# Selected and local attention: the weights turned by TensorE instead of a second pass of scores

## The chip, the cores and the metric

One core of one Trainium2 chip runs the program once. The metric is the time of one execution on the device in microseconds, shown as the median of several runs. One more execution was taken with the hardware profiler; every row below comes from it.

## The reference, cut to what matters

Two transformer blocks follow one another (1024 tokens, width 1024). The first has three mixers: a linear recurrence over 8 heads, a sparse attention with three branches over 4 heads, and an attention over 256 memory rows. The second has retention, a convolution and 64 experts of which each token takes two. The change lies in the sparse attention. With 16 blocks of 64 keys and a top-k of 16, every block is chosen, so the selected branch is causal attention over all earlier keys; the local branch sees the last 512 keys.

```python
s_s = jnp.einsum('bqhd,bqkd->bhqk', qr, kg) * scale
p_s = masked_softmax(s_s, (kpos <= tq[None, :, None])[:, None])
o_s = jnp.einsum('bhqk,bqkd->bqhd', p_s.astype(vg.dtype), vg)
...
m_w = (diff >= 0) & (diff < WINDOW) & (wpos[None, :] >= 0)
s_w = jnp.einsum('bqhd,bkd->bhqk', qr, kwb) * scale
p_w = masked_softmax(s_w, m_w)
o_w = jnp.einsum('bhqk,bkd->bqhd', p_w.astype(vwb.dtype), vwb)
...
o = g[..., 0:1] * o_c + g[..., 1:2] * o_s + g[..., 2:3] * o_w
```

Here 4 heads share one key and value head of 64, and the softmax takes off the largest score of its row.

## The kernel before, in words

The work is staged by halves of the sequence (H is 0 or 1, 512 tokens each). `weave` (L1595) draws from several generators; each `yield` gives a cost, each stream has a rate, and the stream that is furthest behind goes next. Inside a stage the framework then orders each engine's instructions by when it expects them to be ready. L1631 to L1634 weave the projections of the second half with `recur(0)` and `attend(0)`; L1637 weaves `third_stage(0)` (output projection, normalisation, the second block's mixer) with `recur(1)` and `attend(1)`. After them come the second half's output projection and mixer, the router, and the experts, whose weights stream from memory.

`attend` (L1096) takes 4 query tiles of 128 tokens: `mem_tile`, then `nsa_tile` (L947). Values and keys are kept as a float32r high part and a rest: 64 + 64 partitions of `ksT` and `kwT`, 64 + 64 columns of `vsw`; the queries are split into `qh` and `ql` of full value. In `nsa_tile`, per branch (`br`, 0 selected, 1 local) over the key blocks of 128 up to the diagonal (query tile i has i + 1 selected and at most 5 local ones):

- **First pass**, per head and per piece of up to four blocks (`cut`; 5 to 8 blocks make two pieces): scores `pmx` of 128 queries by up to 512 keys (L1012, L1013, masks L1015, L1017), the row's maximum (L1019, DVE), an exponential written back into the same PSUM bank of which only the row sum is kept (L1020, ACT). 96 tiles.
- **Turning the maxima**: 8 maxima per query go through a transpose (`pmr`, L1038) into `nms` and, per branch, into `nmb` (L1044).
- **Second pass**, per key block, all four heads at once: scores `pS` again, now 128 keys by 512 (head, query) (L1057, L1058), less the maximum by a product of `ones` and `nmb` (L1059), a mask on diagonal and edge blocks (L1061). ACT takes the exponential twice, as float32r `ph` (L1064) and as float32 `pf` (L1066); DVE takes `pl` = `pf` - `ph` (L1067); TensorE sums both with the values into `poT` (L1050). 66 blocks.
- **Tail** per branch: the two halves of `poT` are added (L1077, L1078), turned back (`pob`, L1082), weighted and added to `o` (L1085, L1086).

All short-lived score tiles (`pmx`, `pmr`, `pS`, `pob`, those of `mem_tile`) come from `S1` (L217), one ring of two PSUM banks; `poT` has one bank (`O1`). `qd`, `pf` and `mem_tile`'s weights share three buffers of tag `acc`.

Of the kernel before, what the change touches and what calls it, by code (L numbers as in the profile page):

```python
# [9 lines left out]
F32 = mybir.dt.float32  # L10
# [33 lines left out]
def _constants():  # L44

    c = {}
# [19 lines left out]
    r = np.arange(16)[:, None]  # L66
    bh = np.arange(8)[None, :]
    c["nsel"] = np.zeros((P, 8))
    c["nsel"][:16] = 1.0 * (r % 8 == bh)
# [3 lines left out]
    c["causalT"], c["edgeT"] = c["causal"].T, c["edge"].T  # L73
# [18 lines left out]
_GROUPS = (("causal", "edge", "causalT", "edgeT", "before", "ones"), ("ncos", "nsin", "tcos", "tsin", "tcaus", "gam"),  # L92
# [13 lines left out]
def body(tc, a, out, stop=None, dbg=None):  # L106
# [47 lines left out]
    def K(name):  # L154
        o, n = _COFF[name]
        return cst[:, o:o + n]
# [8 lines left out]
    causb, edgeb, causTb, edgeTb, beforeb, onesb = [maskb[:, x * P:(x + 1) * P] for x in range(6)]  # L165
# [184 lines left out]
    def put():  # L350
        return tmp1("put", bufs=3)
# [210 lines left out]
    def att_proj(H):  # L562
        ts, cs = slice(TH * H, TH * H + TH), slice(H2 * H, H2 * H + H2)
        if H == 0:
            for x in range(0, 6, 3):
                masks = put()[:, 0:3 * P]
                nc.sync.dma_start(masks, a["cst"][:, _GOFF[0] + x * P:_GOFF[0] + (x + 3) * P])
                nc.vector.tensor_copy(maskb[:, x * P:(x + 3) * P], masks)
# [311 lines left out]
    nsel = K("nsel")[0:16].rearrange("p (b h) -> p b h", b=2)  # L880

    ones = const.tile([P, P], F32R, name="ones")
    nc.vector.tensor_scalar(ones, ident, 0.0, 1.0, op0=OP.mult, op1=OP.add)
    nmb = at.tile([P, 4, P], F32R, tag="nmb", name="nmb")
    nc.vector.tensor_scalar(nmb, ident[:, None, :].to_broadcast([P, 4, P]), 0.0, None, op0=OP.mult)

# [20 lines left out]
    def mem_tile(i):  # L907
# [5 lines left out]
        for e in range(2):  # L913
            ps = S1("pM")
            for c in range(2):
                nc.tensor.matmul(ps[:, c * 256:(c + 1) * 256], mq[lohi[e], c], memk[lohi[e], c], start=True, stop=True)
            nc.vector.tensor_reduce(nm[:, 2 * e:2 * e + 2], ps.rearrange("p (c k) -> p c k", c=2), axis=AX.X, op=OP.max,
                                    negate=True)
            pr = at.tile([P, 2, 256], F32, tag="acc", name="prm", bufs=3)
# [27 lines left out]
    def nsa_tile(i):  # L947
        H = i // TH
        qd = at.tile([P, 4 * P], F32, tag="acc", name="qd", bufs=3)
# [49 lines left out]
        mx = at.tile([P, 2, 4, 2], F32, tag="mx", name="mx")  # L999
        sm = at.tile([P, 2, 4, 2], F32, tag="sm", name="sm")  # L1000
        for br, kT in enumerate((ksT, kwT)):
# [3 lines left out]
            for h in range(4):  # L1005
                q = slice(h * P, (h + 1) * P)
                for n, (u, v) in enumerate(zip(cut, cut[1:])):
                    ps = S1("pmx")
                    w = (v - u) * P
                    ends, starts = v == nb, br == 1 and i >= 4 and u == 0  # L1010
                    rhs = kT[:, (s0 + u) * P:(s0 + v) * P]
                    nc.tensor.matmul(ps[:, 0:w], qh[:, q], rhs, start=True, stop=False)  # L1012
                    nc.tensor.matmul(ps[:, 0:w], ql[:, q], rhs, start=False, stop=not (ends or starts))  # L1013
                    if starts:
                        nc.tensor.matmul(ps[:, 0:P], identb, edgeb, start=False, stop=not ends)  # L1015
                    if ends:
                        nc.tensor.matmul(ps[:, w - P:w], identb, causb, start=False, stop=True)  # L1017
                    m = mx[:, br, h, n:n + 1]
                    nc.vector.tensor_reduce(m, ps[:, 0:w], axis=AX.X, op=OP.max, negate=True)  # L1019
                    nc.scalar.activation(ps[:, 0:w], ps[:, 0:w], AF.Exp, bias=m, accum_out=sm[:, br, h, n:n + 1])  # L1020
                yield 0.25 * nb
            if len(cut) > 2:
                m, mb = at.tile([P, 4], F32, tag="mc", name="m"), mx[:, br]
                nc.vector.tensor_tensor(m, mb[:, :, 0], mb[:, :, 1], op=OP.min)
                nc.vector.tensor_tensor(mb, m[:, :, None].to_broadcast([P, 4, 2]), mb, op=OP.subtract)
                nc.scalar.activation(mb, mb, AF.Exp)
                nc.vector.tensor_tensor(sm[:, br], sm[:, br], mb, op=OP.mult)
                nc.vector.tensor_tensor(sm[:, br, :, 0], sm[:, br, :, 0], sm[:, br, :, 1], op=OP.add)
                nc.vector.tensor_copy(mb[:, :, 0], m)

        mm = at.tile([P, 2, 8], F32R, tag="mm", name="mm")
        mv = mx[:, :, :, 0]
        nc.vector.tensor_copy(mm[:, 0].rearrange("p (b h) -> p b h", b=2), mv)
        nc.vector.tensor_sub(mm[:, 1].rearrange("p (b h) -> p b h", b=2), mv,
                             mm[:, 0].bitcast(F32).rearrange("p (b h) -> p b h", b=2))
        yield 0.2
        pt = S1("pmr")
        nc.tensor.transpose(pt[0:16, 0:P], mm.bitcast(F32).rearrange("p x n -> p (x n)"), ident)  # L1038
        nms = at.tile([16, P], F32, tag="qn", name="nms")
        nc.vector.tensor_copy(nms, pt[0:16, 0:P])  # L1040
        yield 0.204
        for br, kT in enumerate((ksT, kwT)):
            s0 = b0 if br else 0
            nc.vector.tensor_tensor(nmb[0:16], nms[:, None, :].to_broadcast([16, 4, P]),  # L1044
                                    nsel[:, br, :, None].to_broadcast([16, 4, P]), op=OP.mult)
            po = O1("poT")

            def with_v(b, ph, pl):
                for p_ in (ph, pl):
                    nc.tensor.matmul(po, vsw[:, b, br], p_, start=(b == s0 and p_ is ph), stop=(b == i and p_ is pl))  # L1050

            ready = None
            for b in range(s0, i + 1):
                ps = S1("pS")
                blk = kT[:, b * P:(b + 1) * P]
                mask = causTb if b == i else edgeTb if br == 1 and b == i - 4 else None
# [3 lines left out]
                if mask is not None:  # L1060
                    nc.tensor.matmul(ps.rearrange("p (h t) -> p h t", h=4), identb,  # L1061
                                     mask[:, None, :].to_broadcast([P, 4, P]), start=False, stop=True)
                ph = at.tile([P, 4 * P], F32R, tag="ph", name="ph", bufs=2)
                nc.scalar.activation(ph, ps, AF.Exp)  # L1064
                pl, pf = at.tile([P, 4 * P], F32R, tag="pl", name="pl", bufs=2), at.tile([P, 4 * P], F32, tag="acc", name="pf", bufs=3)
                nc.scalar.activation(pf, ps, AF.Exp)  # L1066
                nc.vector.tensor_sub(pl, pf, ph.bitcast(F32))  # L1067
                yield 0.8
                if ready:
                    with_v(*ready)  # L1070
                    yield 0.604
                ready = b, ph, pl
            yield 0.73
            with_v(*ready)
            yield 0.336
            oS = at.tile([P, 4 * P], F32R, tag="pl", name="oS", bufs=2).bitcast(F32)
            nc.scalar.activation(oS[64:P], po[64:P], AF.Copy)  # L1077
            nc.vector.tensor_tensor(oS[0:64], po[0:64], oS[64:P], op=OP.add)  # L1078
            yield 0.153
            pt = S1("pob")  # L1080
            for h in range(4):
                nc.tensor.transpose(pt[:, h * 64:h * 64 + 64], oS[0:64, h * P:(h + 1) * P], ident[0:64, 0:64])  # L1082
            v = pt[:, 0:256].rearrange("p (h d) -> p h d", h=4)
            t = at.tile([P, 4, 64], F32, tag="sqh", name="ob")
            nc.vector.tensor_tensor(t, v, weight(br + 1, sm[:, br, :, 0]), op=OP.mult)  # L1085
            nc.vector.tensor_tensor(o, o, t, op=OP.add)  # L1086
# [92 lines left out]
    def close_first(H, wk, wg=None):  # L1179
# [3 lines left out]
        for i, rr in enumerate(rows):  # L1183
            n = TH * H + i
            nc.vector.scalar_tensor_tensor(rr, rr, row_rs(wk, rr), gf, op0=OP.mult, op1=OP.mult)
# [3 lines left out]
            nc.scalar.activation(rr, rr, AF.Copy, scale=row_rs(wk, rr))  # L1189
# [822 lines left out]
```

## Time and profile before

| what | us |
|---|---|
| median of 3 runs (2540.53 to 2549.47) | 2548.81 |
| the profiled execution, its own time | 2546.94 |
| its span, from the first to the last instruction | 2544.8 |
| PE busy | 2423.5 |
| DVE busy | 1550.0 |
| ACT busy | 772.7 |
| POOL busy | 348.5 |

PE is busy for 95% of the span, but a matmul's row lasts until its modelled end, which overlaps the next one's start. What a matmul takes from the engine's time is therefore read from one start to the next in a timeline. From 1560 us on the experts run, with the DMA engines busy most of the time.

### The profile page before, as it was taken

The page shows a single profiled execution, that of the slowest core. Times are in us where ns is not written, and L with a number is a line of the kernel's source. Part 1 is how long each engine was busy: PE and PEld are TensorE (multiplying, and loading weights), DVE is VectorE, ACT ScalarE, POOL GpSimd, SP SyncE. Part 2 cuts the span into 40 slices and gives each one's busy share as a digit, 9 for nine tenths or more (in the row PEclk, how much of TensorE's full clock was granted, in tenths as well). Part 3 has the DMA queues.
Part 4 walks back from the last instruction along what each step waited for, and adds up shares of the span by engine and source line. Part 5 has one row for each costly group of instructions (what it writes and reads, how often), then busy time and mean ns, then how long its engine had stood idle before and what let it go on. Part 6 is the DMA issues. An engine that isn't in the chain of part 4 may idle for free. (4 is left out here: it accounts for less than half of the span.)

```text
span 2544.8 us, 36038 instructions
## 1 busy us (share of the span) xinstructions
PE 2423.5 (95%) x13518; PEld 1545.9 (61%) x13518; DVE 1550.0 (61%) x3104; ACT 772.7 (30%) x1516; POOL 348.5 (14%) x464
## 2 busy tenths in 40 slices
PE   8989999999988999999999969999999999999997
PEld 6766777777756767887878834444444444444443
DVE  5537666665776776676665646555555555555555
ACT  4423544434436543334242321111111111111112
POOL 3000000000001011101120020111111111111112
PEclk9989999999888999999999979999999999999999
DMA  7666544443523222445345668999999999999992
GB/s 166 163 148 192 144 106 123 109 121 94 177 59 117 73 70 71 133 136 170 116 139 196 248 237 358 410 408 412 412 409 412 410 408 412 410 410 408 408 410 84
DMA packets 352078, 603.67 MB, mean 237 GB/s; under 512 B 124408, under 2 KB 298112, under 8 KB 327328
## 3 DMA queue, kind: packets, MB, share of 16 engines
q1 hardware_dynamic: 344496, 592.53, 64.9%
q0 software_dynamic: 5168, 8.69, 1.1%
q8 instruction: 108, 1.77, 0.3%
q14 instruction: 66, 0.54, 0.1%
q10 hardware_dynamic: 2240, 0.14, 0.1%
HBM read 562.54 MB, written 47.25 MB: 240 GB/s over the span
## 5 line engine op out<-in xcount | busy, mean ns | idle before, releaser
L1738 PE MATMUL pgu<-mw,xT 128*64 128x512 f32 x2048 | 460.9, 597 | 2.3 <-DVE up L1743 2.3
L277 PE MATMUL pcm<-hTh,whi 128*128 128x512 f32 (+1 forms) x912 | 370.1, 406 | 0.2 <-DVE hTl L265 0.2
L277 PE MATMUL pcm<-hTh,wlo 128*128 128x512 f32 (+1 forms) x912 | 362.9, 398 | 0.4 <-DVE wlo L238 0.4
L277 PE MATMUL pcm<-hTl,whi 128*128 128x512 f32 (+1 forms) x912 | 360.8, 396 | 0.0
L237 ACT ACTIVATE whi<-wraw 128x512 fp32r<-128x512 f32 (+1 forms) x300 | 187.2, 625 | 458.8 <-PE pcm L277 318.0
L238 DVE TENSOR_TENSOR wlo<-wraw,whi 128x512 fp32r<-128x512 f32 (+1 forms) x300 | 211.4, 708 | 181.0 <-ACT whi L237 159.2
L1738 PEld LDWEIGHTS pgu<-mw,xT 128*64 128x64 f32 x2048 | 142.7, 137 | 265.6 <-issue 254.7
L1796 DVE TENSOR_TENSOR mw<-psp,mw 128x1024 f32<-128x1024 f32 x248 | 292.5, 1220 | 8.8 <-PE psp L1788 5.1
L1788 PE MATMUL psp<-yo,wt 128*128 128x512 f32 x1024 | 274.9, 410 | 4.1 <-DVE mw L1796 3.2
L1788 PEld LDWEIGHTS psp<-yo,wt 128*128 128x128 f32 x1024 | 182.8, 188 | 139.0 <-issue 80.6
L1766 PE MATMUL pyd<-mw,hT 128*64 128x512 f32 x1008 | 229.9, 598 | 2.3 <-DVEq L1929 2.3
L1742 DVE SCALAR_TENSOR_TENSOR mth<-mth,pgu 64x512 f32<-64x512 f32 x64 | 43.4, 679 | 291.6 <-ACT mth L1741 291.6
L277 PEld LDWEIGHTS pcm<-hTh,whi 128*128 128x128 f32 (+1 forms) x912 | 170.6, 187 | 41.4 <-issue 6.2
L277 PEld LDWEIGHTS pcm<-hTl,whi 128*128 128x128 f32 (+1 forms) x912 | 170.8, 187 | 39.3 <-issue 6.2
L277 PEld LDWEIGHTS pcm<-hTh,wlo 128*128 128x128 f32 (+1 forms) x912 | 170.2, 187 | 40.1 <-issue 2.3
L1741 ACT ACTIVATE mth<-pgu,rq 64x512 f32<-64x512 f32 x64 | 43.8, 684 | 491.8 <-PE pgu L1738 491.8
L1773 ACT ACTIVATE yo<-pyd,gt 64x512 fp32r<-64x512 f32 x128 | 87.6, 684 | 305.6 <-PE pyd L1766 304.3
L1775 DVE SCALAR_TENSOR_TENSOR yo<-pyd,gt,yo 64x512 fp32r<-64x512 f32 x128 | 95.9, 749 | 126.5 <-ACT yo L1773 125.4
L1781 POOL TENSOR_SCALAR wt<-rcon,tfs 128x128 fp32r<-128x128 f32 x256 | 150.3, 608 | 149.1 <-PE psp L1788 125.4
L1766 PEld LDWEIGHTS pyd<-mw,hT 128*64 128x64 f32 x1008 | 66.9, 136 | 126.7 <-issue 123.2
L1800 POOL DMA_INDIRECT xg<-d_x,idxt x32 | 34.4, 1074 | 688.6 <-issue 630.4
L1170 PE MATMUL pout<-whi,yh 128*128 128x512 f32 x256 | 107.7, 421 | 3.0 <-DVE rr L1173 3.0
(492 smaller groups left out, 3464.3 us busy)
## 6 DMA issues: line engine op xcount, KB each, us to landing
mw<-in_w_gate_dram SPq DMA_DIRECT2D x64, 2048.0 KB, 13.7
mw<-in_w_up_dram SPq DMA_DIRECT2D x64, 2048.0 KB, 9.6
mw<-in_w_down_dram SPq DMA_DIRECT2D x63, 2048.0 KB, 14.4
wraw<-in_w_in_dram SPq DMA_DIRECT2D x216, 256.0 KB, 3.2
wraw<-in_w_out_dram SPq DMA_DIRECT2D x32, 256.0 KB, 2.8
yr<-d_y SPq DMA_DIRECT2D x32, 256.0 KB, 3.0
d_x<-rr SPq DMA_DIRECT2D x16, 512.0 KB, 2.8
wraw<-in_w_o_dram SPq DMA_DIRECT2D x32, 256.0 KB, 2.9
```

Source lines behind the costliest of these rows:

```text
L237: nc.scalar.activation(hi, raw, AF.Copy)
L238: nc.vector.tensor_sub(lo, raw, hi.bitcast(F32))
L277: nc.tensor.matmul(ps[0:n], w, h[:, k], start=(k == 0 and j == 0), stop=(k == KD - 1 and j == 2))
L1170: nc.tensor.matmul(ps, y[:, t], w, start=(k == 0 and j == 0), stop=(k == 1 and j == 2))
L1738: nc.tensor.matmul(ph_[lohi[s]], xT[:, k], pieces[s][:, k * 512:(k + 1) * 512], start=(k == 0), stop=(k == KD - 1))
L1741: nc.scalar.activation(th, ph_[0:64], AF.Tanh, scale=rq[:, 0, h:h + 1])
L1766: nc.tensor.matmul(py[s][lohi[s]], hT[:, k, lohi[h]], piece[:, k * 1024 + s * 512:k * 1024 + s * 512 + 512], start=(k == 0), stop=(k == 3))
L1773: nc.scalar.activation(y[:, 0, 512 * s:512 * s + 512], py[s][o], AF.Copy, scale=gt[o, h:h + 1])
L1775: nc.vector.scalar_tensor_tensor(y[:, 1, 512 * s:512 * s + 512], py[s][o], gt[o, h:h + 1], y[:, 0, 512 * s:512 * s + 512].bitcast(F32), op ...
L1781: nc.gpsimd.tensor_scalar(w[0:n, i], iota[0:n], sh[0:n, i:i + 1], None, op0=OP.is_equal)
L1788: nc.tensor.matmul(ps[:, cs], w[0:n], yo[0:n, x, cs], start=(start and x == 0), stop=(x == 1))
L1796: nc.vector.tensor_tensor(x2, ps, x2, op=OP.add)
```

## The change

The second pass goes. Per branch, piece of up to four key blocks and pair of heads, the exponential of the first pass is now kept, as `pr` in SBUF; TensorE turns it, 128x128 at a time and up to four (two key blocks by two heads) to a bank (`pTs`); ACT copies the bank as float32r `ph`, DVE takes `pl` = `pTs` - `ph`; and TensorE sums both with the values into `poT`, 256 columns at a time. Each piece has its own sum; a piece's `poT` is copied whole, turned by four 128x128 transposes, and its two halves are added after that. Where a branch has two pieces, they are weighted by their own maxima at the end. `ones`, `nmb`, `nsel`, the turned masks and the transpose of the maxima go. `acc` has four buffers; the squares of `close_first` write to tag `yl`; the masks come in one load instead of two. Rates in `weave` are as they were.

```diff
-            for x in range(0, 6, 3):
-                masks = put()[:, 0:3 * P]
...
+            masks = put()
+            nc.sync.dma_start(masks, a["cst"][:, _GOFF[0]:_GOFF[1]])
+            nc.vector.tensor_copy(maskb, masks)
...
-    ones = const.tile([P, P], F32R, name="ones")
...
-    nmb = at.tile([P, 4, P], F32R, tag="nmb", name="nmb")
...
-                    nc.scalar.activation(ps[:, 0:w], ps[:, 0:w], AF.Exp, bias=m, accum_out=sm[:, br, h, n:n + 1])
-                yield 0.25 * nb
...
-        nc.tensor.transpose(pt[0:16, 0:P], mm.bitcast(F32).rearrange("p x n -> p (x n)"), ident)
...
-            for b in range(s0, i + 1):
-                ps = S1("pS")
...
-                nc.tensor.matmul(ps, blk, qh, start=True, stop=False)
-                nc.tensor.matmul(ps, blk, ql, start=False, stop=False)
-                nc.tensor.matmul(ps, ones, nmb.rearrange("p h t -> p (h t)"), start=False, stop=mask is None)
...
-                nc.scalar.activation(ph, ps, AF.Exp)
...
-                nc.scalar.activation(pf, ps, AF.Exp)
-                nc.vector.tensor_sub(pl, pf, ph.bitcast(F32))
...
-            nc.scalar.activation(oS[64:P], po[64:P], AF.Copy)
-            nc.vector.tensor_tensor(oS[0:64], po[0:64], oS[64:P], op=OP.add)
...
+            for n, (u, v) in enumerate(zip(cut, cut[1:])):
...
+                po = O1("poT")
+                ready = []
+
+                def with_v():
+                    j, bs, parts = ready.pop(0)
+                    for k, b in enumerate(bs):
+                        for p_ in parts:
+                            nc.tensor.matmul(po[:, 256 * j:256 * j + 256], vsw[:, s0 + u + b, br], p_[:, 256 * k:256 * k + 256],
+                                             start=(b == 0 and p_ is parts[0]), stop=(b == v - u - 1 and p_ is parts[1]))
+                    return 0.302 * len(bs)
+
+                for j in range(2):
+                    prs = []
+                    for h in (2 * j, 2 * j + 1):
...
+                        ps = S1("pS")
...
+                        nc.vector.tensor_reduce(m, ps[:, 0:w], axis=AX.X, op=OP.max, negate=True)
+                        pr = at.tile([P, 4 * P], F32, tag="acc", name="pr", bufs=4)
+                        nc.scalar.activation(pr[:, 0:w], ps[:, 0:w], AF.Exp, bias=m, accum_out=sm[:, br, n, h:h + 1])
+                        prs.append(pr)
...
+                    for g in range(0, v - u, 2):
+                        bs = range(g, min(g + 2, v - u))
+                        pt = S1("pTs")
+                        for k, b in enumerate(bs):
+                            for x in range(2):
+                                nc.tensor.transpose(pt[:, (2 * k + x) * P:(2 * k + x + 1) * P], prs[x][:, b * P:(b + 1) * P],
+                                                    ident)
+                        c = 256 * len(bs)
+                        ph, pl = [at.tile([P, 4 * P], F32R, tag=t, name=t, bufs=2) for t in ("ph", "pl")]
+                        nc.scalar.activation(ph[:, 0:c], pt[:, 0:c], AF.Copy)
+                        nc.vector.tensor_sub(pl[:, 0:c], pt[:, 0:c], ph[:, 0:c].bitcast(F32))
...
+                nc.scalar.activation(oS, po, AF.Copy)
...
+                for h in range(4):
+                    nc.tensor.transpose(pt[:, h * P:(h + 1) * P], oS[:, h * P:(h + 1) * P], ident)
...
+                nc.scalar.activation(t, pt[:, :, 0], AF.Copy)
+                nc.vector.tensor_tensor(t, pt[:, :, 1], t, op=OP.add)
...
+            jk = dict(tag="yl", bufs=4)
+            nc.vector.scalar_tensor_tensor(rr, rr, row_rs(wk, rr, **jk), gf, op0=OP.mult, op1=OP.mult)
```

Counted over the program, TensorE loses 198 float32r products of 512 columns (132 scores, 66 with `ones`), 20 masks of 512, 8 transposes `pmr` and 64 small transposes `pob`; 132 products with the values of 512 columns become 264 of 256; 264 transposes `pTs` and 96 `pob` of 128x128 come in. ACT loses 132 exponentials and 16 half copies, and gets 78 copies `ph` (54 of 512 columns, 24 of 256), 24 copies of `poT` and 24 of `pob`.

**First place: query tile 7, the products with the values, on PE.** Before, a stretch of the second pass of the selected branch (`pS` scores, `poT` sum, `ph` and `pl` the two parts of the weights):

```order
L1057 MATMUL pS<-qh,ksT 128x512
L1058 MATMUL pS<-ql,ksT 128x512
L1050 MATMUL poT<-pl,vsw 128x512
L1059 MATMUL pS<-nmb,ones 128x512
L1050 MATMUL poT<-ph,vsw 128x512
L1057 MATMUL pS<-qh,ksT 128x512
```

In the changed kernel, whose own line numbers stand here, the same branch (`pTs` the turned weights, `pcm` a projection of the second block):

```order
L1032 MATMUL pTs<-cst,pr 128x128 x7
L272 MATMUL pcm<-hTh,wlo 128x512
L1004 MATMUL poT<-ph,vsw 128x256
L272 MATMUL pcm<-hTh,whi 128x512
L272 MATMUL pcm<-hTl,whi 128x512
L272 MATMUL pcm<-hTh,wlo 128x512
L1004 MATMUL poT<-pl,vsw 128x256
```

Where one block's scores stood between another block's weights and their products, seven transposes stand ahead, and projections stand between.

**Second place: query tile 7, scores of one head and the next, on PE.** Before, two tiles of the first pass:

```order
L1012 MATMUL pmx<-ksT,qh 128x512
L1013 MATMUL pmx<-ksT,ql 128x512
L277 MATMUL pcm<-hTh,wlo 128x512
L277 MATMUL pcm<-hTh,whi 128x512
L277 MATMUL pcm<-hTl,whi 128x512
L1012 MATMUL pmx<-ksT,qh 128x512
L1013 MATMUL pmx<-ksT,ql 128x512
```

In the changed kernel, the second head of a pair and the transposes that need its exponential (`pZ` and `pY` are the recurrence):

```order
L1013 MATMUL pS<-ksT,qh 128x512
L1014 MATMUL pS<-ksT,ql 128x512
L816 MATMUL pY<-E,UV 128x128
L814 MATMUL pZ<-UV,E 128x128
L816 MATMUL pY<-E,UV 128x128
L272 MATMUL pcm<-hTh,whi 128x512
L1032 MATMUL pTs<-cst,pr 128x128
L272 MATMUL pcm<-hTl,whi 128x512
L272 MATMUL pcm<-hTh,wlo 128x512
L272 MATMUL pcm<-hTh,whi 128x512
L272 MATMUL pcm<-hTl,whi 128x512
L1032 MATMUL pTs<-cst,pr 128x128 x7
```

Before, the next score tile needs only a free bank; now, the seven transposes need the exponential of the scores at the top, with three small products, one transpose and five projections in between.

## Rows read from the trace of the kernel before

**Rows 1.** Windows by stage: busy us (and instructions) of PE, PEld, DVE, ACT, POOL; clock; DMA.

```profile
308.00:637.00 329.00, 320.71 (x2200) 241.61 (x2198) 206.81 (x469) 144.79 (x313) 26.41 (x21) 0.99 0.43 109
637.00:976.00 339.00, 315.71 (x2123) 226.73 (x2123) 245.22 (x592) 171.04 (x395) 28.46 (x27) 0.93 0.32 96
...
1560.00:2544.00 984.00, 957.66 (x4288) 433.06 (x4286) 546.00 (x791) 152.97 (x231) 185.63 (x296) 1.00 0.94 387
```

**Rows 2.** Issues of the expert weights: ns min/median/max, first and last start, forms.

```profile
L1676 SPq DMA_DIRECT2D mw<-in_w_gate_dram x64: 327/328/1042, 1337.8 to 2459.2; - x64
```

**Rows 3.** Waits of PE, 308 to 976 us: us in total, times, longest.

```profile
PE pfin L900 <- DVE on L896: 5.7, 4, 3.8
PE pfin L900 <- DVE om L896: 5.4, 5, 3.3
PE pmx L1012 <- ACT pmx L1020: 3.4, 7, 1.0
PE pmr L1038 <- DVE nrs L190: 3.3, 1, 3.3
...
PE pob L1082 <- DVE oS L1078: 0.9, 2, 0.6
```

**Rows 4.** Timeline of PE, steady second pass, query tile 7: start, us, what.

```profile
949.57 0.45 PE L1057 MATMUL pS<-qh,ksT 128*128 128x512 f32 x1
949.86 0.39 PE L1058 MATMUL pS<-ql,ksT 128*128 128x512 f32 x1
950.09 0.39 PE L1059 MATMUL pS<-nmb,ones 128*128 128x512 f32 x1
950.32 0.43 PE L1050 MATMUL poT<-pl,vsw 128*128 128x512 f32 x1
950.59 0.39 PE L1050 MATMUL poT<-ph,vsw 128*128 128x512 f32 x1
```

**Rows 5.** Timeline of PE: products of 256 columns; then float32 transposes and what follows.

```profile
264.47 0.28 PE L653 MATMUL pmk<-hTl,whi 128*128 128x256 f32 x1
264.59 0.28 PE L653 MATMUL pmk<-hTh,wlo 128*128 128x256 f32 x1
...
899.77 0.66 PE L930 MATMUL pTm<-cst,prm 128*128 128x128 f32 x4
900.35 0.54 PE L750 MATMUL pE<-AR,BK 64*64 64x192 f32 x4
900.83 0.50 PE L277 MATMUL pcm<-hTh,whi 128*128 128x512 f32 x1
901.17 0.40 PE L277 MATMUL pcm<-hTl,whi 128*128 128x512 f32 x1
901.40 0.49 PE L930 MATMUL pTm<-cst,prm 128*128 128x128 f32 x3
901.73 0.33 PE L937 MATMUL pom<-memv,pTm 128*128 128x64 f32 x2
```

**Rows 6.** Groups by line and shape, 308 to 976 us: busy, mean ns | idle before.

```profile
L1067 DVE TENSOR_TENSOR pl<-pf,ph 128x512 fp32r<-128x512 f32 x66 | 45.6, 690 | 38.8 <-ACT pf L1066 34.5 <-PE pS L1059 3.5 <-PE pS L1058 0.5
L1064 ACT ACTIVATE ph<-pS 128x512 fp32r<-128x512 f32 x66 | 39.6, 600 | 44.4 <-PE pS L1059 28.9 <-PE pS L1061 15.0
L1066 ACT ACTIVATE pf<-pS 128x512 f32<-128x512 f32 x66 | 39.5, 599 | 0.0
...
L1020 ACT ACTIVATE pmx<-pmx,mx 128x512 f32<-128x512 f32 x20 | 13.2, 659 | 11.2 <-DVE mx L1019 10.9 <-DVE ri L190 0.2
...
L921 ACT ACTIVATE prm<-pM,nm 128x256 f32<-128x256 f32 x28 | 13.0, 471 | 25.9 <-DVE nm L917 25.9
...
L1020 ACT ACTIVATE pmx<-pmx,mx 128x256 f32<-128x256 f32 x28 | 12.3, 440 | 4.3 <-DVE mx L1019 4.1
...
L1078 DVE TENSOR_TENSOR oS<-poT,oS 64x512 f32<-64x512 f32 x16 | 10.9, 682 | 5.2 <-ACT oS L1077 4.9
L1044 DVE TENSOR_TENSOR nmb<-nms,cst 16x512 fp32r<-16x512 f32 x16 | 10.8, 672 | 0.9 <-PE pS L1059 0.9
...
L1077 ACT ACTIVATE oS<-poT 64x512 f32<-64x512 f32 x16 | 9.5, 593 | 16.0 <-PE poT L1050 15.9
...
L1085 DVE TENSOR_TENSOR ob<-pob,den 128x256 f32<-128x256 f32 x16 | 6.8, 423 | 9.3 <-PE pob L1082 8.3 <-PE pa L428 0.8
```

**Rows 7.** Timeline of all engines, first scores of tile 7.

```profile
916.88 0.23 PE L1017 MATMUL pmx<-maskb,identb 128*128 128x128 bf16 x1
...
917.36 0.41 DVE L996 TENSOR_TENSOR on<-on,den 128x256 f32<-128x256 f32 x1
...
917.69 0.68 DVE L1019 TENSOR_REDUCE mx<-pmx 128x1 f32<-128x512 f32 x1
...
918.47 0.66 ACT L1020 ACTIVATE pmx<-pmx,mx 128x512 f32<-128x512 f32 x1 [0.15 <-DVE ri L190]
```

More of the change, by code (lines that the diff above doesn't have):

```diff
@@ L89, in _constants @@
     return c
-_GROUPS = (("causal", "edge", "causalT", "edgeT", "before", "ones"), ("ncos", "nsin", "tcos", "tsin", "tcaus", "gam"),
+_GROUPS = (("causal", "edge", "before", "ones"), ("ncos", "nsin", "tcos", "tsin", "tcaus", "gam"),
            ("iota", "slotv"))
@@ L164, in body @@
     maskb = const.tile([P, _GOFF[1] - _GOFF[0]], BF, name="maskb")
-    causb, edgeb, causTb, edgeTb, beforeb, onesb = [maskb[:, x * P:(x + 1) * P] for x in range(6)]
+    causb, edgeb, beforeb, onesb = [maskb[:, x * P:(x + 1) * P] for x in range(4)]
     mhalf = const.tile([P, 64], F32, name="mhalf")
@@ L879, in body @@
     cokt, cnegt = K("cok"), K("cneg")
-    nsel = K("nsel")[0:16].rearrange("p (b h) -> p b h", b=2)
-    ones = const.tile([P, P], F32R, name="ones")
-    nc.vector.tensor_scalar(ones, ident, 0.0, 1.0, op0=OP.mult, op1=OP.add)
-    nmb = at.tile([P, 4, P], F32R, tag="nmb", name="nmb")
-    nc.vector.tensor_scalar(nmb, ident[:, None, :].to_broadcast([P, 4, P]), 0.0, None, op0=OP.mult)
     def finish_heads(i, o, x):
@@ L918, in mem_tile @@
                                     negate=True)
-            pr = at.tile([P, 2, 256], F32, tag="acc", name="prm", bufs=3)
+            pr = at.tile([P, 2, 256], F32, tag="acc", name="prm", bufs=4)
             for c in range(2):
@@ L948, in nsa_tile @@
         H = i // TH
-        qd = at.tile([P, 4 * P], F32, tag="acc", name="qd", bufs=3)
+        qd = at.tile([P, 4 * P], F32, tag="acc", name="qd", bufs=4)
         nc.sync.dma_start(qd, d_q[i].rearrange("q h t -> q (h t)"))
@@ L997, in nsa_tile @@
         yield 0.5
-        mx = at.tile([P, 2, 4, 2], F32, tag="mx", name="mx")
-        sm = at.tile([P, 2, 4, 2], F32, tag="sm", name="sm")
+        mx = at.tile([P, 2, 2, 4], F32, tag="mx", name="mx")
+        sm = at.tile([P, 2, 2, 4], F32, tag="sm", name="sm")
         for br, kT in enumerate((ksT, kwT)):
@@ L1004, in nsa_tile @@
             cut = [0, nb] if nb <= 4 else [0, (nb + 1) // 2, nb]
[L1005 to L1019, printed above, removed]
-                    nc.scalar.activation(ps[:, 0:w], ps[:, 0:w], AF.Exp, bias=m, accum_out=sm[:, br, h, n:n + 1])
-                yield 0.25 * nb
@@ L1087, in nsa_tile @@
+                nc.vector.tensor_tensor(m, sm[:, br, 0], sm[:, br, 1], op=OP.add)
+                weight(br + 1, m)
+                for n, t in enumerate(outs):
+                    nc.vector.tensor_tensor(mb[:, n], mb[:, n], den[:, :, br + 1], op=OP.mult)
+                    nc.vector.tensor_tensor(t, t, mb[:, n, :, None].to_broadcast([P, 4, 64]), op=OP.mult)
+            for t in outs:
+                nc.vector.tensor_tensor(o, o, t, op=OP.add)
         yield from finish_heads(i, o, 0)
```

92 lines of the change are left out of this document (35 added, 57 removed).

## The prediction

> **What bounds the kernel now.** I read the windows by stage first. The reader is to see that attention runs in two stages, 308 to 637 us and 637 to 976 us. PE is busy for 320.71 of 329 us in the first and for 315.71 of 339 us in the second, and the granted clock is 0.99 and 0.93 [rows 1]. DVE has 245.22 us of work in the second stage, ACT 171.04: neither is full. So PE bounds both stages; in the second it also loses 339 - 315.71 = 23.3 us idle, and a clock that averages 0.93 between the levels 2.4 and 1.2 GHz means 0.14 of 339 us, 47 us, at 1.2 GHz, in which some 24 us are lost. Next come the waits of PE. The longest, 5.7 and 5.4 us, are for the last normalisation of a tile, which the change leaves alone; the waits that it touches are 3.4 us for a bank of the first pass, 3.3 us before the turning of the maxima and 0.9 us before `pob` [rows 3]. Then the timeline: in the steady second pass a product of 512 columns starts every 0.23 us (949.86, 950.09, 950.32) although its row lasts 0.39 [rows 4]. There PE never waits. The second pass is thus TensorE's own time, with ACT (two exponentials, 1.2 us a block [rows 6]) about level with five products (1.17 us).
>
> **What a saving is worth at the end.** The experts follow at a DMA share of 0.94 [rows 1], but their first weights are issued at 1337.8 us [rows 2], behind results that come after attention. What attention saves or loses moves that stream, and the end, by as much.
>
> **The parts, on PE, start to start at 2.4 GHz.**
> - Gone: 198 products of 512 columns at 0.23 us, 45.5 us; 20 masks, taken as one such product each, 4.6; 132 products with the values, 30.4; 72 small transposes at the 0.12 us taken below, 8.6, and 0.11 for the change of mode (below) behind each of 16 groups, 1.8. Together 91 us.
> - Added: 264 products of 256 columns. One starts 0.12 us after another (264.47, 264.59) [rows 5]: 31.7 us. Two halves cost 0.24 where one whole cost 0.23, so halving is nearly free.
> - Added: 264 + 96 transposes of float32 blocks. No row shows such long runs of them. Four took 900.35 - 899.77 = 0.58 us, 0.145 each; three took 901.73 - 901.40 = 0.33, 0.11 each [rows 5]. I take 0.12, near the lower end, because seven stand in a row in the new order: 43.2 us; the ends are 39.6 and 52.2.
> - Added: behind a float32 group the first float32r product takes 0.34 us to the next (900.83 to 901.17) in place of 0.23 [rows 5]. The new order enters transposes twice per pair of heads, 48 pairs, and 24 times for `pob`: 120 times 0.11, 13.2 us.
> - Sum on PE: 31.7 + 43.2 + 13.2 - 91 = -3 us. With the gone transposes priced alike, the ends are -6 and +4.
>
> **The parts on ACT and DVE.** ACT loses 39.6 + 39.5 + 9.5 = 88.6 us [rows 6]. It gets 54 copies of 512 columns at 0.600, 24 copies of `poT` at 0.593, and 48 copies of 256 columns, which I price at the 0.440 us of an exponential of that size [rows 6]: 32.4 + 14.2 + 21.1 = 67.7. That is 21 us less. DVE loses 45.6 + 10.9 + 10.8 us and 32 operations of 256 columns at 0.42 (13.4), with some 6 us of small ones; it gets 54 differences at 0.69, 24 at 0.42, 72 operations of 256 columns at 0.42 and 4 us of small ones, 81.6 in all: 5 us less. Both lie beside PE's work. They count only where PE waits for these engines, between nothing and the whole 23.3 us that PE is idle in the second stage. I take 4 us, what is left of the touched waits being so small.
>
> **Where the exponential is written.** The 96 exponentials of the first pass now go to SBUF instead of PSUM. The rows have 0.440 us for 256 columns into PSUM and 0.471 into SBUF [rows 6]: 0.03 times 96, 3 us of ACT's 21, not on PE's path. The Trainium skill, "PSUM — Partial Sum Buffer", Specifications, says that ScalarE writes faster to PSUM than to SBUF, a rule against the change; the rows agree. By the rule alone ACT would gain less than 21 us; by the rows it gains 18, and the sum stays.
>
> **The waits that come in.** Before, PE met the weights a block late; now the first seven transposes of a pair need the second head's exponential. Two dependencies count.
> - Scores to transposes. In the trace the last score product of the second tile starts at 916.88 and its exponential ends at 918.47 + 0.66 = 919.13 [rows 7]: 2.25 us. The new order puts between them (second place in the section on the change) five projections (1.15 us), four small products (some 0.5): 0.6 us short in a tile of four blocks. Narrower tiles need less. Upper end 48 times 0.6, 29 us; lower end nothing, if the framework leaves enough in between elsewhere.
> - Transposes to products. `ph` takes 0.60 us with hand-overs of 0.1 (918.37 to 918.47 [rows 7]) on both sides, 0.8; between stand four transposes and one projection, 0.7. `pl` takes 0.69 and a hand-over; between stand three projections, 0.69. Short by 0.1 each, at most 10 us.
> - Behind the waiting instruction the projections, the recurrence and the output projection queue; all of PE's streams stop, and nobody else runs ahead.
> - I take a quarter of the 39 us, 10, because the old first pass had the same length of chain through two banks, 96 times, with as little in between, and shows 3.4 us of waits in all. From that go the 3.4 and 3.3 us [rows 3] that end with the old passes: +3.
>
> **Edits at nothing.** One load of masks instead of two, `ones` and `nmb` no longer set: under 2 us of DVE in the stages before. The squares of `close_first` write into buffers whose last readers, the products of the output projection, are done before the row is complete; without that cover each of 16 squares would wait about one product, 4 us. No transfer is moved past another on a queue that anybody waits for.
>
> **Sum.** -3 + 3 - 4 = -4 us: from the profiled execution's 2546.94 us to 2543 us. The median of the runs shown lies 1.9 us above that execution, so against the median I say 2544 us. This is no change: about 0.5%, 12.7 us, is what a measurement of this kernel can tell.
>
> **The rivals.**
> - *The relief is larger* (faster). If fewer operations on ACT and DVE shorten the idle time of the second stage and keep the clock up, both losses there (23.3 and 24 us) could fall by a third, 16 us, and with the transposes at their lower price (-6) the time is 2547 - 22 = 2525. For it: the second stage has DVE at 245.22 of 339 us and the lower clock [rows 1], and the new order has more projections inside attention. Against it: the longest waits there are not touched [rows 3].
> - *Two banks hold up PE* (slower). Scores, turned weights and turned sums share the ring of two banks. A pair's scores fill both, its turned weights fill both again, and each must be emptied by two operations in series before PE may go on; before, the ring let PE run a block ahead. With the whole 39 us of shortage, the transposes at 0.145 (+4) and the 6.7 us that go, the time is 2547 + 36 = 2583; at two thirds of the shortage and the taken price of transposes, 2547 + 26 - 7 - 3 = 2563. It decides from about 0.5 us of wait per pair. For it: an instruction seldom finds DVE free at once; the second reduction, whose scores were issued at 916.88, starts behind another instruction at 917.69 [rows 7]. Against it: the 3.4 us. The Trainium skill, "Perfetto Trace Analysis", Identifying Performance Opportunities, says that the same gap recurring on the engine that should be full can mean too little PSUM for the next tile; the trace of before shows no such gap, that of after would.
> - *The gain or loss does not reach the end.* If the experts' stream did not move with attention, the time would be 2547. The first issue [rows 2] speaks against it, and it would be no change as well.
>
> **How the numbers follow.** No change, sum and third rival together: 0.46, with 2534 to 2560 as its own range. Faster by over 0.5%: 0.32, nearly all of it the first rival; the nearest prices are within 10 us of the border, so I give it more than the waits alone would. Slower by over 0.5%: 0.22, the second rival. The range takes in 2525 and 2563 and goes a little beyond both, 2522 to 2567; the full price of the banks, 2583, is left out with about 1 in 10.
>
> **What would show it.** In the changed profile: 264 `pTs` of about 0.12 us start to start, 264 `poT` of 256 columns at 0.12; ACT's sum down by about 20 us, DVE's by about 5; PE's waits for `pr`, `ph` and `pl` near 10 us in all; stages of attention as long as before within 10 us each; the experts' first issue near 1334. Waits of over 25 us at the transposes or at `poT` would show the second rival; a clock over 0.95 in the second stage with less idle time would show the first. A change of more than 13 us with neither would mean that the orders around attention, which I took as equal, decide.

## The result and the profile after

| | before | changed |
|---|---|---|
| median of 7 runs, us | 2548.66 | 2561.12 |
| ratio, 95% interval | | 1.0056 [1.0041, 1.0071] |
| span of the profiled execution, us | 2544.8 | 2555.6 |
| ACT busy, DVE busy, us | 772.7, 1550.0 | 753.3, 1538.6 |

The change makes the kernel slower by about 0.56%, 12.5 us between the medians and 10.8 between the two profiled spans. That is the side of the rival "two banks hold up PE" (2563), not of the forecast (2544).

The windows by stage of the changed kernel, with the columns of [rows 1]. The first row is the first half of attention, from its first `pfin` to its last; the second has the bounds of the second row of [rows 1]; the third is the second half, from the last `pfin` of the first half to the last `pr` of the recurrence; the fourth lies inside it.

```profile
316.60:636.60 320.00, 308.35 (x2189) 236.62 (x2188) 190.84 (x442) 134.47 (x298) 25.02 (x20) 0.98 0.42 110
...
637.00:976.00 339.00, 310.34 (x2227) 234.48 (x2227) 233.85 (x570) 147.80 (x350) 29.35 (x26) 0.87 0.33 98
636.60:1055.80 419.20, 387.63 (x2878) 294.61 (x2878) 287.03 (x700) 176.37 (x415) 41.75 (x36) 0.90 0.30 90
...
740.00:800.00 60.00, 47.48 (x279) 34.36 (x278) 38.62 (x103) 30.80 (x63) 7.23 (x9) 0.63 0.33 103
```

The same stretches of the kernel before, between the same events:

```profile
318.20:636.60 318.40, 310.12 (x2141) 232.92 (x2140) 201.65 (x458) 140.72 (x306) 25.39 (x20) 0.99 0.44 111
636.60:1045.30 408.70, 382.92 (x2723) 279.12 (x2723) 286.44 (x680) 189.09 (x429) 40.14 (x36) 0.94 0.31 92
740.00:800.00 60.00, 49.85 (x285) 35.34 (x285) 40.74 (x108) 36.53 (x80) 5.42 (x8) 0.78 0.34 106
```

The first half begins 1.6 us earlier in the changed kernel and ends at 636.6 us in both. The second is 10.5 us longer, nearly the whole of the 10.8 us between the spans. In the second half PE is idle for 419.20 - 387.63 = 31.6 us in place of 25.8, and the granted clock averages 0.90 in place of 0.94. Stretches of 4 us of the changed kernel show what PE did when the clock fell:

```profile
724.00:728.00 4.00, 1.67 (x5) 1.23 (x5) 3.73 (x12) 0.00 (x0) 1.01 (x1) 0.74 0.00 0
728.00:732.00 4.00, 4.00 (x10) 2.54 (x10) 2.76 (x8) 0.83 (x4) 0.00 (x0) 0.50 0.12 33
...
740.00:744.00 4.00, 1.11 (x6) 0.62 (x5) 3.10 (x11) 0.26 (x1) 1.63 (x1) 0.87 0.23 62
744.00:748.00 4.00, 4.00 (x12) 2.87 (x12) 2.57 (x9) 0.00 (x0) 0.00 (x0) 0.50 0.12 33
748.00:752.00 4.00, 1.52 (x7) 0.98 (x5) 2.49 (x8) 0.49 (x2) 0.00 (x0) 0.50 0.22 66
```

PE is busy for 1.67 of 4 us and then runs at 1.2 GHz; again 1.11 of 4 us, and then 1.2 GHz with one short recovery until about 788 us. Here the output projection of the first half ends in a serial piece (PE stands idle for 3.30 us before a product that waits for `rr` at 726.33 us, and for 2.48 us at 751.95), and attention, which itself waits for `om` for 2.89 us at 743.87, is nearly all that PE has beside it.

The experts' first weights [rows 2] move with attention, by 10.1 us:

```profile
L1662 SPq DMA_DIRECT2D mw<-in_w_gate_dram x64: 327/334/512, 1347.9 to 2470.0; - x64
```

The waits of PE from 306 to 1016 us (waiting instruction, what it waited for, us in total, times, longest), to be set against [rows 3]:

```profile
PE pfin L887 <- DVE on L883: 9.0, 6, 4.4
PE pfin L887 <- DVE om L883: 7.9, 5, 3.3
PE pout L1155 <- DVE rr L1158: 6.5, 4, 3.3
PE pTs L1032 <- ACT pr L1022: 4.9, 9, 1.9
PE poT L1004 <- ACT ph L1036: 3.7, 7, 1.3
PE pob L1050 <- ACT oS L1046: 1.6, 2, 1.2
PE poT L1004 <- DVE pl L1037: 1.5, 2, 1.2
```

The new waits (`pTs`, `poT`, `pob`) are 4.9 + 3.7 + 1.6 + 1.5 = 11.7 us; the waits for `pmx` and `pmr` are gone. By this list the second rival would have failed: it was to show over 25 us. The groups of the new instructions, 306 to 1016 us, with the columns of [rows 6]:

```profile
L1037 DVE TENSOR_TENSOR pl<-pTs,ph 128x512 fp32r<-128x512 f32 x54 | 36.3, 688 | 16.2 <-ACT ph L1036 15.9
...
L1036 ACT ACTIVATE ph<-pTs 128x512 fp32r<-128x512 f32 x54 | 31.1, 595 | 18.9 <-PE pTs L1032 18.7
...
L1022 ACT ACTIVATE pr<-pS,mx 128x512 f32<-128x512 f32 x20 | 13.7, 685 | 15.9 <-DVE mx L1020 15.9
...
L1022 ACT ACTIVATE pr<-pS,mx 128x256 f32<-128x256 f32 x28 | 13.2, 472 | 13.8 <-DVE mx L1020 13.5
...
L1036 ACT ACTIVATE ph<-pTs 128x256 fp32r<-128x256 f32 x24 | 9.1, 379 | 1.3 <-PE pTs L1032 1.3
```

### The profile page after: what moved, and what is told of

Same layout as the page of the kernel before. It is cut to its first block, busy times and chain, and to the rows that moved or that the text cites. A ratio compares the mean times of both kernels' runs of the same rounds, so it can differ in the third digit from the quotient of the medians.

```text
span 2555.6 us, 36296 instructions
## 1 busy us (share of the span) xinstructions
PE 2424.8 (95%) x13720; PEld 1564.0 (61%) x13720; DVE 1538.6 (60%) x3105; ACT 753.3 (29%) x1494; POOL 349.8 (14%) x464
```

## The experiments

Three theories stood at first, and a fourth came after the first four runs. **P**: the framework that orders the instructions puts attention later among the projections (its last tile ends at 1636 projection products in PE's order, before at 1566), where PE runs short. **W**: the waits listed above are the loss. **U**: the loss comes from the first half or the small edits. **B** (the fourth): the chain of a pair of heads through two PSUM banks is held up, wherever it stands. A ratio is against the kernel before on the same chip. That kernel took 2544.80 to 2546.75 us there and 2548.66 above, so results are compared by their ratios; a difference of two ratios is uncertain by 4 to 6 us as a rule. Each kernel has one profile, of a single execution, and its windows carry an argument only where the ratios agree with them.

**A third bank in the second half.** The bank `v` serves nobody there until 862 us. The ring becomes first bank of `s`, `v`, second bank of `s`.

```diff
-    ring = {"J": ["pj"], "V": ["v"]}
+    ring = {"J": ["pj"], "V": ["v"], "S": ["s"]}
...
-        return ps_tile("s", name)
+        return ring_tile("S", name)
...
     g0 = third_stage(0)
+    ring.update(S=["s", "v", "s"])
```

> The changed kernel, with the bank `v` as a third member of the ring of `S1` in the second half of attention alone. Theory P (place): in the changed kernel the chain of a pair of heads through two banks is so long that other streams' instructions were put ahead of it on PE; attention stands up to 76 projection products later in PE's order, its thin parts (end of one tile, start of the next) meet the thin end of the first output projection at 720 to 790 us, PE runs short and the granted clock falls to half; this, and not the waits, is the cost. With the third bank the order has the second half's first tile end at 120 output products in place of 153 and the last one at 1609 projections in place of 1636, so the spells at half clock get shorter: 2546 to 2554 us. Theory W (waits): the waits of PE at `pTs` and `poT` themselves are the cost (7.9 us in the stage); with a third bank they fall under 3 us and the time by about 5 us, to 2556. Theory U (upstream): the loss comes from the other edits or the first half; no change from 2561.

Measured: 2541.47 us, 0.9986 [0.9976, 0.9995]. One bank takes the loss back, and some more than any theory allowed. The second half, and 740 to 800 us, in its windows:

```profile
637.70:1038.20 400.50, 378.18 (x2874) 286.55 (x2874) 284.25 (x699) 175.12 (x411) 40.01 (x36) 0.94 0.32 94
740.00:800.00 60.00, 55.11 (x472) 41.86 (x470) 46.82 (x118) 40.47 (x92) 5.40 (x9) 0.94 0.39 117
```

With the same instructions the second half is 419.2 - 400.5 = 18.7 us shorter. PE's idle time is 22.3 us in place of 31.6, which is 9.3 of it; the rest goes with the clock, 0.94 for 0.90. The ratios agree: from 1.0056 to 0.9986, 18 us. The listed waits at `pTs`, `poT` and `pob` fall only by 6.2 us in this half (9.7 to 3.5), so W can't carry it. Why a bank matters is seen in the order of PE. The changed kernel, start of the second half's first tile (timeline of PE):

```profile
664.16 0.44 PE L1013 MATMUL pS<-ksT,qh 128*128 128x384 f32 x1 [0.35 <-ACT on L973]
...
666.59 0.27 PE L1032 MATMUL pTs<-cst,pr 128*128 128x128 f32 x1
...
667.17 0.71 PE L1032 MATMUL pTs<-cst,pr 128*128 128x128 f32 x5
667.63 0.48 PE L1155 MATMUL pout<-whi,yh 128*128 128x512 f32 x1
667.95 0.40 PE L1155 MATMUL pout<-wlo,yh 128*128 128x512 f32 x1
668.18 0.40 PE L1155 MATMUL pout<-whi,yl 128*128 128x512 f32 x1
668.74 0.39 PE L1004 MATMUL poT<-ph,vsw 128*128 128x256 f32 x1 [0.16 <-ACT ph L1036]
...
669.67 0.28 PE L1004 MATMUL poT<-pl,vsw 128*128 128x256 f32 x1
669.79 0.28 PE L1004 MATMUL poT<-ph,vsw 128*128 128x256 f32 x1
669.91 0.28 PE L1004 MATMUL poT<-pl,vsw 128*128 128x256 f32 x1
670.02 0.34 PE L1013 MATMUL pS<-ksT,qh 128*128 128x384 f32 x1
```

The same place with three banks:

```profile
663.57 0.44 PE L1013 MATMUL pS<-ksT,qh 128*128 128x384 f32 x1
...
666.27 0.38 PE L1032 MATMUL pTs<-cst,pr 128*128 128x128 f32 x2
...
666.96 0.60 PE L1032 MATMUL pTs<-cst,pr 128*128 128x128 f32 x4
667.32 0.42 PE L1013 MATMUL pS<-ksT,qh 128*128 128x384 f32 x1
```

With two banks the next pair's scores come behind the products, 670.02 - 664.16 = 5.9 us after the first pair's; with three they stand right behind the transposes, 667.32 - 663.57 = 3.75 us. PE hardly waits in either: with two banks it takes products of the output projection (`pout`) in between. That this work is then missing later is argued, not shown (see the place alone, and the useless work). Over the sixteen pieces of the second half the distance from the first pair's scores to the second's sums to 97 us with two banks and to 72 with three.

The Trainium skill, "Perfetto Trace Analysis", Optimizing Tensor Performance, says that independent groups of products should go round different PSUM banks, so that emptying one overlaps the next group's products. The 18.7 us agree.

**The place alone.** The kernel before, one number changed, and the third bank in about the changed kernel's place:

```diff
-          (attend(1), 0.1, 0.554), until=(1, 2))
+          (attend(1), 8.1, 0.554), until=(1, 2))
```

> The kernel before, with one number changed: attention of the second half enters the interleaving 8 us later (8.1 in place of 0.1). In PE's order its tiles then end at 159 output products and at 1426, 1512 and 1591 projections, near the places they have in the changed kernel (153, 1431, 1543, 1636). No arithmetic differs. Theory P: the place alone makes the loss; the granted clock falls in 740 to 790 us as in the changed kernel, 2556 to 2564 us. Theories W and U: nothing that the change did is in this kernel, 2549 us within 4.

Measured: 2549.23 us, 1.0017 [1.0003, 1.0032]: about a third of the loss, by the interval at most some three fifths.

> The third bank, with attention of the second half entering the interleaving 5 us later (5.1 in place of 0.1), so that its tiles end in PE's order at 144 output products and at 1424, 1521 and 1637 projections, about where the changed kernel has them with two banks (153, 1431, 1543, 1636). Theory P (place): the place decides whatever the banks, so most of the third bank's gain is lost again: 2552 to 2562 us. Theory B (the hold-up in the chain itself): where the instructions stand matters little; what matters is that PE no longer stands behind evictions of two banks, and then the clock holds too: 2540 to 2547 us, as with the third bank in its own place.

Measured: 2541.49 us, 0.9981 [0.9968, 0.9993]. Late attention with three banks is as fast as early attention with three banks: P falls as the main cause, B holds, but not in the clock: between 740 and 800 us this profile (an execution of 2548.22 us, the slowest of ten) has 0.79, hardly more than the 0.78 of the kernel before, and the kernel is not slow.

**The third bank with an earlier turn** (`attend(1), 0.1, 0.40`).

> The third bank, and attention of the second half at a rate of 0.40 in place of 0.554 in the interleaving, which gives it the earlier turn. In PE's order its tiles then end at 120 output products and at 1392, 1464 and 1560 projections, as in the kernel before or earlier. Theory P: what the change saves on PE in the second half (about 12 us at full clock) is kept, since the clock is as before: 2535 to 2546 us, below the third bank alone. Theory W: as the third bank alone, about 2556. Theory U: 2561.

Measured: 2540.9 us, 0.9987 [0.9972, 1.0002], no better than the bank alone, again against P. PE's listed wait at `pTs` for `pr` was 7.0 us in the second half of this run, where the changed kernel has 4.7: the list is no measure of the loss.

**The first half alone** (the new pass where `H == 0`, the old ones elsewhere).

> The kernel before, with the new pass in the first half of the sequence alone (8 of the 24 pieces), three buffers for `acc`, and the old squares of `close_first`. Theory P: the second half stands in PE's order as before (126 output products, 1486 and 1560 projections), so there is no loss: 2545 to 2551 us. Theory W: a third of the waits, about 2552 us. Theory U, as far as it is the first half: 2555 us or more.

Measured: 2549.33 us, 1.0012 [1.0002, 1.0022]. The first half with two banks costs some 3 us (0.5 to 5.6 by the interval), a fifth of the loss; U is no more than that part.

**The edit of `close_first` undone** (`row_rs(wk, rr, **jk)` is `row_rs(wk, rr)` again).

> The changed kernel with one of its small edits undone: the squares of `close_first` write into their own buffer again. Theories P and B: the edit has nothing to do with the loss, 2558 to 2564 us. Theory U (the small edits): the squares now wait for buffers of the output projection (rows of 3.3 us before the output products), and without the edit the time falls by 8 us or more, to 2553 or below.

Measured: 2564.31 us, 1.0092 [1.0064, 1.0120]. Without the edit nothing is won; U falls.

**Useless work in the thin places.**

```diff
+    def fill(x, n=16):
+        dm = V1("dm")
+        r = x.bitcast(BF)
...
+            nc.tensor.matmul(dm[:, 0:256], identb, r[:, 1:512:2], start=True, stop=True)
```

> The changed kernel with useless work added on PE: at six places of tiles 4 to 7 where its order is thin (the end of one tile and the start of the next), 16 products of 256 columns in bfloat16 each, 96 in all, about 11 us of PE at full clock, into the bank `v` that nobody reads then; the output is unchanged. Theory C (the clock carries the loss, and it falls because PE runs short there): the stretches at half clock in 720 to 790 and 925 to 945 us get shorter by half, which gives back some 15 us, and the added work costs 6 to 11: 2552 to 2562 us, in spite of more work. If the clock is only a companion of the loss: 2568 to 2580 us.

Measured: 2561.59 us, 1.0074 [1.0054, 1.0094], which overlaps the changed kernel's interval. The difference of 0.0018 is 5 us, uncertain by 6: the 96 products may have cost nothing or their whole 11 us. Between 740 and 800 us the clock is 0.80 in place of 0.63:

```profile
740.00:800.00 60.00, 49.90 (x381) 37.72 (x381) 43.98 (x117) 34.13 (x72) 6.51 (x9) 0.80 0.34 106
```

The low clock there goes with PE's lack of work, since work that does nothing else raises it. What it costs is not shown: the filling brought no time back that can be told, and the third bank with late attention is fast at 0.79. It is a companion of the loss and may carry a part of it; it is not its origin.

**Which use of the bank counts.** Either the turned weights of the second half go into `v` alone (`pt = (V1 if H else S1)("pTs")`), or they stay in the two banks of `s` and all else goes round three (`pt = ps_tile("s", "pTs")`).

> The changed kernel with the turned weights `pTs` of the second half in the bank `v`, and everything else in the two banks of `s` as before. Theory B (a pair's scores, its turned weights and the next pair's scores follow one another through two banks, so that the next pair's scores come only behind this pair's products): the scores of the next pair may now be taken while the turned weights are emptied, so most of the third bank's gain is there, 2541 to 2549 us. But two groups of turned weights of one pair share one bank then; if the hold-up lies there, between the groups, the gain is small: 2553 to 2561 us.

Measured: 2570.09 us, 1.0087 [1.0062, 1.0113], slower than either expectation although it has one bank more than the changed kernel. Its timeline shows the second group of turned weights waiting until the first has left the single bank (all engines, rows between left out):

```profile
762.34 0.59 ACT L1036 ACTIVATE ph<-pTs 128x512 fp32r<-128x512 f32 x1
...
763.38 0.68 DVE L1037 TENSOR_TENSOR pl<-pTs,ph 128x512 fp32r<-128x512 f32 x1
...
764.21 0.41 PE L1032 MATMUL pTs<-cst,pr 128*128 128x128 f32 x2 [0.84 <-DVE pl L1037]
```

> The kernel with the third bank, but with the turned weights kept to the two banks of `s`: only scores, sums and the rest go round three banks. Theory B: the next pair's scores find a bank of their own in one case of two only and the turned weights again share with scores, so it lies between the two: 2543 to 2553 us. If what matters is that the scores run ahead, whatever bank the turned weights have: 2540 to 2545 us.

Measured: 2542.29 us, 0.9977 [0.9963, 0.9991], as the second expectation has it. In these runs it is enough that the two groups of turned weights alternate and that the next pair's scores have somewhere to go. How long attention lasts shows the two sides: the products of `pl` with the values in the second half, first and last start, of the changed kernel, the third bank, the turned weights in `v` alone, and the turned weights kept to `s` (the three figures after `x92` are durations in ns):

```profile
L1004 PE MATMUL poT<-pl,vsw x92: 274/282/582, 669.7 to 1009.4; 128*128 128x256 f32 x92
L1004 PE MATMUL poT<-pl,vsw x92: 276/281/562, 669.1 to 974.2; 128*128 128x256 f32 x92
L1004 PE MATMUL poT<-pl,vsw x92: 274/283/581, 672.8 to 1014.8; 128*128 128x256 f32 x92
L1004 PE MATMUL poT<-pl,vsw x92: 274/282/582, 672.8 to 968.9; 128*128 128x256 f32 x92
```

340 and 342 us in the slow kernels, 305 and 296 in the fast ones. The distance between the scores of two pairs alone is no such measure: with the turned weights in `v` alone it sums to 46 us, the shortest, and that kernel is the slowest.

**Three banks in both halves, and the old first half.** `narrow` sets the same ring for the first half; and, apart, the old passes where `H == 0` with the bank in the second half alone.

> The third bank in both halves. In the first half PE has other work at every moment (idle 10 us of 331 and clock 0.98 with two banks), and the bank `v` serves the mixer's projections there. Theory B: the hold-up costs only where PE has nothing else, so the first half gains nothing: 2539 to 2545 us, as with the bank in the second half alone. If the hold-up costs everywhere: 2528 to 2536 us.

Measured: 2536.12 us, 0.9955 [0.9943, 0.9967]. The expectation of B for the first half was wrong: it gains too. Its first half and second half:

```profile
320.90:633.60 312.70, 304.13 (x2193) 231.75 (x2191) 190.92 (x443) 135.50 (x302) 24.96 (x20) 0.99 0.43 112
...
633.60:1035.90 402.30, 379.64 (x2874) 287.56 (x2874) 284.35 (x699) 175.04 (x411) 40.04 (x36) 0.93 0.31 93
```

The first half is 320.0 - 312.7 = 7.3 us shorter, though the waits listed there had been under 3 us. But 4.3 us of this is its start, which comes later in this execution (320.9 against 316.6 us); it ends 3.0 us earlier. By the ratios, 0.9986 with the bank in the second half alone and 0.9955 here, the gain is 8 us, uncertain by 4.

> The old two passes in the first half, the new pass with the third bank in the second half; three buffers for `acc` and the old squares. The new pass in the first half alone cost 0.12% (3 us); if that adds up, this kernel is the fastest: 2536 to 2541 us. If the first half is worth nothing either way: 2540 to 2544 us.

Measured: 2535.17 us, 0.9950 [0.9934, 0.9966]. Faster than both kernels, and level with three banks in both halves. Against the new first half with two banks (0.9986) the old one is 9 us faster here, uncertain by 5, where the run with the first half alone had priced it at 3.

**The same banks for the old passes.**

> The kernel before, with the bank `v` as a third member of the ring of `S1` in the second half, and nothing of the change. If the bank is what the change needed and the old passes did not (their listed waits for banks are 3 to 4 us): 2541 to 2547 us. If a third bank is worth as much to the old passes as to the new one (19 us): 2526 to 2534 us, and the change itself is a loss with three banks too.

Measured: 2541.77 us, 0.9999 [0.9987, 1.0012].

> The kernel before with three banks in both halves, to be set against the changed kernel with three banks in both halves (2536 us, 0.9955). If the sum of the prediction holds where banks are not short (TensorE saves a few us), the old passes stay above the new one: 2540 to 2547 us. If the third bank in the first half is worth 5 us to any kernel, as the new pass showed: 2534 to 2539 us, and the change is worth nothing of itself.

Measured: 2546.94 us, 1.0010 [0.9998, 1.0022]. A third bank is worth nothing to the old passes. Between equals, three banks on both sides, the change goes from 1.0010 to 0.9955: it is worth some 14 us, uncertain by 4.

> Old passes in the first half, new pass in the second, three banks in both. If the old first half is held up by banks too: 2529 to 2533 us, the fastest so far. If not: 2534 to 2538 us, as with the bank in the second half alone (0.9950).

Measured: 2536.05 us, 0.9966 [0.9950, 0.9982]: no gain over the bank in the second half alone.

**The price of the transposes**, on the kernel with three banks in both halves:

```diff
-                                nc.tensor.transpose(pt[:, (2 * k + x) * P:(2 * k + x + 1) * P], prs[x][:, b * P:(b + 1) * P],
-                                                    ident)
+                                for _ in range(1 + H):
+                                    nc.tensor.transpose(pt[:, (2 * k + x) * P:(2 * k + x + 1) * P],
+                                                        prs[x][:, b * P:(b + 1) * P], ident)
```

> The changed kernel with three banks in both halves, and every transpose of the turned weights of the second half made twice into the same place (184 more; the output is unchanged). If TensorE bounds that half and one costs 0.12 us, as in the prediction's sum: 22 us more, 2556 to 2560 us. At the 0.09 us that the changed kernel's rows show from start to start in groups of four: 16 us more, 2551 to 2554 us. If TensorE has room there: under 8 us more, below 2544 us.

Measured: 2545.38 us, 1.0003 [0.9991, 1.0016], so 0.0048 or 12 us over the kernel without the doubling, uncertain by 4: 0.04 to 0.09 us for each of 184, between two expectations. This is no price of a transpose: the rows give 0.11 (next section), 20 us for 184, and in the profiles the second half is only 407.5 - 402.3 = 5.2 us longer, at a granted clock of 0.96 in place of 0.93. Part of the added transposes fell where PE had room.

## Why the prediction was wrong

- **The waits that come in** is the step that failed. It found the right places and a shortage of 39 us at most, and took a quarter, 10 us, because the old first pass showed 3.4 us. With three banks in both halves the ratio goes from 1.0056 to 0.9955: the hold-up was worth about 26 us, uncertain by 5, some 18 of it in the second half. That is two thirds of the 39, which is what the second rival was priced with. The old first pass was the wrong model: its tiles go through the two banks once, a pair's scores and then its turned weights go through them twice. The list of waits did not show the price (11.7 us), since "nobody else runs ahead" was wrong: PE's order was built with other streams' products put into the hold. The loss shows in the second half as idle time (31.6 us in place of 22.3 with the third bank) and as a lower clock (0.90 for 0.94). How the hold turns into that time stays open. That spent `pout` products are what is missing at 740 us is not shown: the changed kernel has spent 153 of them at the end of the half's first tile, the kernel before with late attention 159 and the third bank with late attention 144, at a clock of 0.80 and 0.79, and they lose 0.17% and nothing.
- **The sum on PE** was mis-sized the other way. Products of 256 columns at 0.12 us (669.67, 669.79, 669.91) were right. Transposes start (0.71 - 0.27) / 4 = 0.11 us apart, by the row of five and the row of one (667.17, 666.59): the lower end, where 0.12 was taken. The change of mode, put at 13.2 us, is the term that was wrong. The product behind the five does take 0.32 us in place of 0.23 (667.63 to 667.95), but it starts 0.46 us after the first of them, where five times 0.11 are 0.55. Both together, 667.95 - 667.17 = 0.78 us, less the product's own 0.23, leave 0.55 for five transposes, 0.11 each with the change of mode in it. The 39 groups of this trace with a product right behind have 0.11 in the median. So the sum is 31.7 + 39.6 - 88.4 = -17, not -3 (88.4 is the 91 with the gone transposes at 0.11 and no change of mode). Between equals the change is worth 14, uncertain by 4, which bears this out. The Trainium skill, "TensorE: Matmul & The Clock Gate", Part 4, gives about 275 ns for a bf16 transpose of 128x128 in one kernel; a row of one float32 transpose has 0.27 us here, and they start 0.11 us apart, so a duration of one is no price for a run of them.
- Corrected, -17 + 26 = +9 us, against 10.8 us between the spans and 12.5 between the medians; the 26 alone is uncertain by 5.
- **ACT and DVE**: 19.4 us less on ACT, forecast 21 and 18 with the writes to SBUF; these cost 685 and 472 ns where PSUM took 659 and 440 [rows 6], as the rows said. DVE lost 11.4, forecast 5. The relief of 4 us on PE that was taken from it did not come with two banks: PE's idle time grew.
- **What a saving is worth at the end** was right: 10.1 us at the experts' first issue, 10.8 at the end.
- **Edits at nothing**: undoing the squares won nothing; the others were not run alone.
- **The rivals**: the second was the true one by mechanism, with a chance too low at 0.22. That its price came so near (2563 against 2561) is partly luck: it holds the same sum of -3 on PE, 14 us off, and takes off 7 us for waits that end. Its criterion, over 25 us of waits at `pTs` and `poT`, was a bad one. The first rival did not come even where banks are not short: the gain over the kernel before is 0.45% there, 11 us of its 22 and no more than the sum on PE gives, and the granted clock of the second half is 0.93, no higher than before. The order around attention, named as the last resort, moved; its place alone cost about a third of the loss.

## What to carry to other kernels

When a change makes a chain go twice through the same ring of PSUM banks, count who holds each bank until when, and judge it by how long the whole chain lasts (340 us with two banks here, 305 with three), not by the waits of the engine: an order with other work put into the hold keeps it off that list. Before such a change is judged, try it with one bank more, and give the same bank to the old kernel; here the first turned a loss of 0.56% into a gain of 0.45%, and the second changed nothing.

## What was not expected of the hardware

Float32 transposes of 128 x 128 start 0.11 us apart at the full clock although each row lasts 0.27 us, and the change to float32r behind them cost nothing beyond that: the product behind five starts 0.46 us after the first and takes 0.32 us in place of 0.23. And 96 useless products, some 11 us of TensorE at full clock, went with a granted clock of 0.80 in place of 0.63 between 740 and 800 us, at a cost of 5 us, uncertain by 6.
